# The last two places of a mixture of experts cut to 64 tokens, the tokens' rows read ahead of the last weights, and the sum z kept in PSUM

## The chip, the cores and the metric

The kernel runs on one NeuronCore of one Trainium2 chip. The metric is the device time of one execution in microseconds. TensorE is called PE here, VectorE DVE, ScalarE ACT, GpSimd POOL; SP is SyncE, which issues nearly all of the DMAs.

## What is computed

One encoder block over 512 tokens of width 1024: a layer norm, a token mixer (gated linear attention and differential attention), a second norm, a mixture of experts, a third norm. The change lies in the mixture of experts and the third norm:

```python
logits = xf @ router_w + router_b          # 512 tokens, 32 experts
top_v, top_i = lax.top_k(logits, 4)        # 4 experts for a token
gates = softmax(top_v)
# for each expert, over the tokens that chose it:
g = min(x @ w_gate[e] + b_gate[e], 7)
u = clip(x @ w_up[e] + b_up[e], -7, 7)
a = g * sigmoid(1.702 * g) * (u + 1)
yb = a @ w_down[e] + b_down[e]             # all three weights are 1024 x 1024 f32
y[token] += gate * yb
h = LN2(alpha * h + y)
```

## The kernel before

From about 735 us on, the kernel works through 32 **places**, one expert each. Places 0 and 1 hold experts 0 and 1; the other experts are sorted by their number of tokens and put into places of fitting size. A place has a form (`FORM`, line 32). `None` takes 128 tokens, with weights and tokens split into two fp32r parts and three matmuls a product (L1341 to L1343). `(4, 3)`, `(2, 1)` and `(4, 1)` take 96, 64 and 32 tokens in plain fp32, several small matmuls at once in column tiles of the array (L1351). Place 20 (`WIDE`) takes 128 tokens and 32 more.

A place has three **products**, gate, up and down, of eight steps k each; the step of one place runs gate of e, up of e, down of e-1 (`gate_up`, `down`, `product`). Each product begins with a matmul that adds the bias (L1324 for `None`, L1326 for `(2, 1)`, L1330 for the two others), so these rows mark where products begin. Between the steps lie the transposes ("turns") of the activations `u` into `an` (in gate of e, by the form of e-1) and of the gathered tokens `x` into `xn` (in down of e-1, by the form of e+1).

The weights come as **tiles** of 1 MB, two steps k each: four tiles a product, twelve a place, 384 in all, in the order gate e, up e, down e-1. They are listed in `todo` and issued on SP (`load`, L1015) into 12 slots (11 around place 20). A slot is free when PE has done with its tile (`used`, `free_row`), for a `None` place when the tile has been split. So tile n is issued when tile n-12, one place earlier, has been used. Results of a place are scattered to DRAM by token (`scatter`, tensor `s_y`, four rows for each token), except those of the last two places.

**The end before.** After the weights, `todo` holds eight tiles of 1 MB that read `s_y` back (`yv`): for each of the four blocks b of 128 tokens, the rows of choices 2 and 3 first, then those of 0 and 1. `scaled` adds gate times row into the sum z of the block (DVE L1587, or ACT L1584 and POOL L1585), some while the last product runs (`late`), some through PE (`ON_PE`, L1614, with a diagonal matrix `dg`). The results of places 30 and 31 stay on the chip, split in two parts (`y2`: L1422 on ACT, L1423 on DVE), and `add_back` (L1188) spreads them over the tokens with a 0/1 matrix `w`. `combine` adds PSUM into z (L1615), and `finish` normalises: statistics (L1858), root on ACT (L1860), scale (L1866), the affine part (L1873 to L1878), the output. PSUM is handed out in two rings of four banks, `psb` and `psl`.

## Time and profile before

| | us |
|---|---|
| median of 3 runs | 1827.13 |
| lowest and highest run | 1823.83, 1828.16 |
| the profiled execution, its own time | 1825.93 |
| its span, first to last instruction | 1823.9 |
| PE busy | 1731.9 (95%) |
| DVE busy | 705.8 (39%) |
| weights, queue q1: share of 16 DMA engines | 68.7% |

The table counts a whole execution with stages of different limits; the shares say little about the stage that changes, which begins near 890 us. All times below count from the start of the span. A matmul's row lasts longer than the distance to the next one, since matmuls overlap; the distance between starts is what one costs.

### The profile page before, as it was taken

What the parts mean: (1) busy time and instruction counts of PE and PEld (TensorE: products, weight loads), DVE (VectorE), ACT (ScalarE), POOL (GpSimd) and SP (SyncE); (2) the same over time, 40 slices, a digit from 0 to 9 for tenths busy, and PEclk for the clock granted to TensorE, in tenths of its full rate; (3) what the DMA queues carried; (4) which work ended last, traced back from release to release, by engine and by line L of the source; (5) the groups of instructions that cost most, each with busy time, mean ns of one, the idle gap of its engine ahead of it and who ended that gap; (6) DMA issues with size and microseconds to landing.
All of it is one profiled execution on the core that took longest, in us unless ns stands there. A gap on an engine that the chain in (4) does not pass through costs nothing. (4 is left out here: it accounts for less than half of the span.)

```text
span 1823.9 us, 34470 instructions
## 1 busy us (share of the span) xinstructions
PE 1731.9 (95%) x14456; PEld 1139.2 (62%) x14456; DVE 705.8 (39%) x1055; ACT 571.0 (31%) x947; POOL 478.8 (26%) x399
## 2 busy tenths in 40 slices
PE   6899999899899999899999999999999999999995
PEld 5688887678677788775355554545455454454583
DVE  5337647867673456783000000000004300000598
ACT  5523336555553233562101111011114311101472
POOL 4303415654433023561112211020110101101204
PEclk9999999999999999999999999999999999999998
DMA  7233343113433875489999999999999999999992
GB/s 233 101 116 104 127 128 104 52 52 122 142 130 112 295 271 218 156 293 417 419 418 417 418 419 416 418 412 413 402 401 404 394 378 419 418 420 419 421 421 93
DMA packets 111651, 525.06 MB, mean 288 GB/s; under 512 B 15480, under 2 KB 15920, under 8 KB 61700
## 3 DMA queue, kind: packets, MB, share of 16 engines
q1 hardware_dynamic: 97940, 492.05, 68.7%
q0 software_dynamic: 11248, 26.58, 3.9%
q10 hardware_dynamic: 2304, 4.20, 0.6%
q8 instruction: 115, 1.88, 0.4%
q14 instruction: 44, 0.36, 0.1%
HBM read 490.38 MB, written 37.58 MB: 289 GB/s over the span
## 5 line engine op out<-in xcount | busy, mean ns | idle before, releaser
L1351 PE MATMUL psb<-raw,xn 128*32 128x256 f32 (+1 forms) x6400 | 470.7, 402 | 7.6 <-DMA raw<-in_exp_w_up_dram 3.9
L1351 PEld LDWEIGHTS psb<-raw,xn 128*32 128x32 f32 (+1 forms) x6400 | 222.5, 112 | 207.6 <-issue 69.9
L1367 DVE TENSOR_SCALAR u<-psb 128x512 f32<-128x512 f32 (+1 forms) x51 | 30.5, 599 | 679.4 <-PE psb L1351 679.4
L1351 PE MATMUL psl<-raw,an 128*32 128x256 f32 (+1 forms) x3200 | 241.0, 404 | 3.3 <-DMA raw<-in_exp_w_down_dram 3.3
L1351 PEld LDWEIGHTS psl<-raw,an 128*32 128x32 f32 (+1 forms) x3200 | 109.9, 113 | 99.3 <-issue 34.1
L229 PE MATMUL psb<-hTh,wh 128*128 128x512 f32 x384 | 162.1, 422 | 8.2 <-ACT sg L544 4.0
L1232 POOL DMA_INDIRECT x<-s_h,grows x56 | 57.5, 1028 | 422.9 <-PE psl L1278 396.2
L1049 DVE TENSOR_TENSOR wl<-raw,wh 128x1024 fp32r<-128x1024 f32 x114 | 136.9, 1225 | 48.9 <-ACT wh L1038 18.7
L231 PE MATMUL psb<-hTl,wh 128*128 128x512 f32 x384 | 153.7, 400 | 0.0
L230 PE MATMUL psb<-hTh,wl 128*128 128x512 f32 x384 | 153.0, 398 | 0.0
L1038 ACT CAST wh<-raw 128x1024 fp32r<-128x1024 f32 x114 | 117.7, 1049 | 67.7 <-PE psb L1342 32.5
L1240 POOL DMA_INDIRECT s_y<-y,srows x53 | 53.6, 1012 | 318.6 <-DMA s_y<-y,srows 159.9
L169 ACT CAST wh<-raw 128x1024 fp32r<-128x1024 f32 x88 | 91.8, 1046 | 129.4 <-PE psb L231 81.2
L1279 ACT COPY xn<-psl 128x512 f32<-128x512 f32 (+1 forms) x41 | 20.4, 497 | 341.5 <-PE psl L1278 341.5
L170 POOL TENSOR_TENSOR wl<-raw,wh 128x1024 fp32r<-128x1024 f32 x36 | 91.5, 2540 | 116.7 <-ACT wh L169 82.3
L170 DVE TENSOR_TENSOR wl<-raw,wh 128x1024 fp32r<-128x1024 f32 x52 | 70.1, 1351 | 92.4 <-ACT wh L169 92.4
L229 PEld LDWEIGHTS psb<-hTh,wh 128*128 128x128 f32 x384 | 73.4, 191 | 27.7 <-ACT sg L544 5.1
L230 PEld LDWEIGHTS psb<-hTh,wl 128*128 128x128 f32 x384 | 73.5, 192 | 18.3 <-issue 2.5
L231 PEld LDWEIGHTS psb<-hTl,wh 128*128 128x128 f32 x384 | 73.1, 190 | 18.7 <-DVE hTl L349 0.9
L1279 ACT COPY an<-psl 128x512 f32<-128x512 f32 (+1 forms) x41 | 20.4, 497 | 162.7 <-PE psl L1278 162.7
L1341 PE MATMUL psb<-wh,xh 128*128 128x512 f32 x160 | 66.4, 415 | 1.2 <-ACT wh L1038 1.2
L1343 PE MATMUL psb<-wl,xh 128*128 128x512 f32 x160 | 64.4, 403 | 3.2 <-DVE wl L1049 3.2
(460 smaller groups left out, 2728.8 us busy)
## 6 DMA issues: line engine op xcount, KB each, us to landing
raw<-in_exp_w_up_dram SPq DMA_DIRECT2D x128, 1024.0 KB, 17.3
raw<-in_exp_w_down_dram SPq DMA_DIRECT2D x128, 1024.0 KB, 17.8
raw<-in_exp_w_gate_dram SPq DMA_DIRECT2D x125, 1024.0 KB, 17.0
raw<-in_w_in_dram SPq DMA_DIRECT2D x32, 1024.0 KB, 6.2
s_y<-zero SPq DMA_DIRECT2D x16, 512.0 KB, 8.0
raw<-s_y SPq DMA_DIRECT2D x8, 1024.0 KB, 19.2
raw<-in_w_br_gla_dram SPq DMA_DIRECT2D x4, 1024.0 KB, 6.5
raw<-in_w_br_diff_dram SPq DMA_DIRECT2D x4, 1024.0 KB, 5.6
```

Source lines behind the costliest of these rows:

```text
L169: nc.scalar.copy(h, raw[:, 2 * s:2 * s + 2])
L170: self.low.tensor_sub(l, raw[:, 2 * s:2 * s + 2], h.bitcast(F32))
L229: nc.tensor.matmul(out, lhsT=sh, rhs=mh, start=first, stop=False)
L230: nc.tensor.matmul(out, lhsT=sl, rhs=mh, start=False, stop=False)
L231: nc.tensor.matmul(out, lhsT=sh, rhs=ml, start=False, stop=last)
L1038: nc.scalar.copy(h, src)
L1049: nc.vector.tensor_sub(sub[2], sub[0], sub[1].bitcast(F32))
L1232: self.nc.gpsimd.indirect_dma_start(out=x[:, t * D // n:(t + 1) * D // n], out_offset=None, in_=self.K.d_h1.rearrange("t (n d) -> (t n) d" ...
L1240: self.nc.gpsimd.indirect_dma_start(out=self.K.d_y.rearrange("t (n d) -> (t n) d", n=n), out_offset=bass.IndirectOffsetOnAxis(ap=srow, axi ...
L1341: nc.tensor.matmul(ps[n], lhsT=xh[:, k], rhs=h[:, cs], start=False, stop=False)
L1343: nc.tensor.matmul(ps[n], lhsT=xh[:, k], rhs=l[:, cs], start=False, stop=k == KC - 1)
L1351: nc.tensor.matmul(ps[t * d // T][i * m:i * m + m, t * d % T:t * d % T + d], lhsT=xT[:, o:o + m], rhs=w[:, i * d:(i + 1) * d], start=False ...
```

## The change

1. **Forms.** The two `None` places at the end (30 and 31) become `(2, 1)`, of 64 tokens. The number of places of each form stays: places 11 and 24, which were `(2, 1)`, become `None`, and the places between are dealt out anew.
2. **Reads of `s_y`.** They stand ahead of the last four weight tiles (down of 31), ordered by block. They may be issued once place 29 has been scattered (`y_there`). Each of the eight read tiles is added to z on DVE by two instructions (`add_rows`), four tiles in up of 31, four in down of 30; then its slot is free for a later load.
3. **z in PSUM.** Within the last product PE takes z of a block into PSUM by a matmul with the identity (`fold_z`) and adds the rows of place 30; after the product, those of 31. The norm reads PSUM. The diagonal matrices, `scaled`, `combine` and the adds on POOL go.
4. **Turn of place 31.** It stands inside down of 30, at k = 3, instead of behind it.

```diff
-for _f, _is in (((4, 1), (2, 19, 29)), ((2, 1), (3, 4, 8, 11, 14, 17, 21, 24, 26, 28)),
-                ((4, 3), (5, 6, 7, 9, 10, 12, 13, 15, 16, 18, 22, 23, 25, 27))):
+for _f, _is in (((4, 1), (2, 19, 29)), ((2, 1), (3, 4, 8, 12, 15, 18, 22, 27, 30, 31)),
+                ((4, 3), (5, 6, 7, 9, 10, 13, 14, 16, 17, 21, 23, 25, 26, 28))):
...
+        self.y_at, self.y_there = self.n_w - N_LAST, False
...
-        while self.n_raw < n and self.free:
-            slot = self.slots[self.n_raw] = self.free.pop(0)
+        while self.n_raw < n and self.free and (self.n_raw != self.y_at or self.y_there):
+
+            i = self.n_raw - self.y_at
+            key = self.n_raw if i < 0 else ("y", i) if i < Y_TILES else self.n_raw - Y_TILES
+            slot = self.slots[key] = self.free.pop(0)
...
-        for n in range(2):
-            for i in range(2):
-                self.nc.tensor.matmul(ps[n], lhsT=w[:, b * P:(b + 1) * P], rhs=y[i][:, n * 512:(n + 1) * 512],
+        for i in range(2):
+            for n in range(2):
+                m, cs = (slice(0, P), slice(n * 512, (n + 1) * 512)) if form is None else (slice(n * 64, n * 64 + 64), slice(0, 512))
+                self.nc.tensor.matmul(ps[n], lhsT=w[m, b * P:(b + 1) * P], rhs=y[i][m, cs],
...
+            if e == E - 3:
+                self.y_there = True
+                self.load()
...
+                if e == E - 1 and which == 1 and k in K_Y0:
+                    add_rows(K_Y0.index(k))
...
-                self.todo += [yv[b][:, j:j + 2] for j in (2, 0) for b in range(NB)]
+                self.todo[self.y_at:self.y_at] = [yv[b][:, j:j + 2] for b in range(NB) for j in (0, 2)]
...
+            def add_rows(i):
+
+                b, y = i // 2, self.raws.pop(("y", i))
+                for j in range(2):
+                    n = i % 2 * 2 + j
+                    nc.vector.scalar_tensor_tensor(self.z[b], y[j], self.gates[:, b, n:n + 1], self.z[b], op0=ALU.mult, op1=ALU.add)
+                self.give(self.slots.pop(("y", i)))
...
+                if k in K_Y:
+                    add_rows(4 + K_Y.index(k))
+                if k == K_LAST:
+
+                    aT = left.tile([P, D], F32, tag="al", bufs=1, name="an")
+                    self.turn_form(us[0], aT, FORM[E - 1])
...
-                self.down(aT, before, E - 2, tail, y2[0], gs[0])
-                aT = self.turn(us[0], "a")
+                self.down(aT, before, E - 2, tail, y2[0], gs[0], FORM[E - 2])
...
+        ps = [[self.psb(), self.psb()] for b in range(2)]
+
+        def fold_z(b, n):
+            nc.tensor.matmul(ps[b][n], lhsT=c.ident, rhs=self.z[b][:, n * 512:(n + 1) * 512], start=True, stop=False)
 
         def late(k):
...
+            if k in K_Z:
+                b = K_Z.index(k)
+                if b == 2:
+                    ps.append([self.psl(), self.psl()])
+                for n in range(2):
+                    fold_z(b, n)
+                self.add_back(ps[b], b, w[:, 0], y2[0], False, False, FORM[E - 2])
+
+        self.down(aT, self.ohs[:, :, E - 1:E], E - 1, late, y2[1], gs[1], FORM[E - 1])
+        ps.append([self.psl(), self.psl()])
+        for n in range(2):
+            fold_z(3, n)
+        self.add_back(ps[3], 3, w[:, 0], y2[0], False, False, FORM[E - 2])
         for b in range(NB):
...
+            self.add_back(ps[b], b, w[:, 1], y2[1], False, True, FORM[E - 1])
+        self.finish(out, [left.tile([P, D], F32, tag=t, bufs=1, name="o" + t) for t in ("g", "s", "ah", "al")], ps)
...
+Y_TILES, N_LAST = 8, 4
...
+K_Y0, K_Y, K_LAST, K_Z = (1, 3, 5, 7), (1, 2, 3, 4), 3, (2, 4, 6)
```

Lines move by up to 16 (L1351 becomes L1357, L1188 L1194, L1015 L1019). How the order of the instructions moves, at three places:

PE at the start of place 24, its gate product. `psb` and `psl` are PSUM, `xn` and `xh`, `xl` the turned tokens, `wh`, `wl` the split weights, `an` the turned activations. Before:

```order
L1326 MATMUL psb<-bias,ohg 128x512
L1351 MATMUL psb<-raw,xn 64x512 x8
L1278 MATMUL psl<-tab,u 128x128 x4
L1351 MATMUL psb<-raw,xn 64x512 x4
L1278 MATMUL psl<-tab,u 128x128 x2
```

and now, the first step of the same product:

```order
L1330 MATMUL psb<-bias,ohs 128x512 x2
L1347 MATMUL psb<-wh,xh 128x512
L1348 MATMUL psb<-wh,xl 128x512
L1349 MATMUL psb<-wl,xh 128x512
L1347 MATMUL psb<-wh,xh 128x512
```

Place 24 has become a `None` place in the middle of the run, six matmuls a step in place of two.

SP at the end of the list of loads. Before:

```order
L1015 DMA raw<-in_exp_w_down_dram 128x2048
L1015 DMA raw<-s_y 128x2048 x8
L1874 DMA out_dram<-og 128x1024
L1874 DMA out_dram<-os 128x1024
L1874 DMA out_dram<-oah 128x1024
```

and now (the rows of register arithmetic between the last loads are left out):

```order
L1019 DMA raw<-in_exp_w_down_dram 128x2048
L1019 DMA raw<-s_y 128x2048 x8
...
L1019 DMA raw<-in_exp_w_down_dram 128x2048
...
L1891 DMA out_dram<-og 128x1024
L1891 DMA out_dram<-os 128x1024
```

The eight reads of `s_y` now have the four tiles of down of 31 behind them.

PE from the turn of place 31 to the last add. `y`, `x` are the two parts of place 30's result, `wh`, `wl` those of place 31's. Now:

```order
L1284 MATMUL psl<-tab,u 128x128 x4
L1357 MATMUL psl<-raw,an 64x512 x8
L1332 MATMUL psl<-bias,ohg 128x512
L1357 MATMUL psl<-raw,an 64x512 x6
L1607 MATMUL psb<-z_4743,tab 128x512 x2
L1194 MATMUL psb<-y,w 128x512 x2
L1194 MATMUL psb<-x,w 128x512 x2
L1357 MATMUL psl<-raw,an 64x512 x4
```

The folds of z and the adds of place 30 now lie between the steps of the last product; before, PE had nothing but that product there, and all 32 adds (L1188) behind it.

## Rows read from the trace of the kernel before

**Rows 1.** The page: what the DMA moved in 40 equal slices of the span.

```profile
GB/s 233 101 116 104 127 128 104 52 52 122 142 130 112 295 271 218 156 293 417 419 418 417 418 419 416 418 412 413 402 401 404 394 378 419 418 420 419 421 421 93
```

**Rows 2.** Waits of PE from 893.5 to 1679 us: us in total, times, longest.

```profile
PE psl L1330 <- ACT ohg L1312: 0.5, 1, 0.5
PE psb L1351 <- DMA raw<-in_exp_w_gate_dram: 0.4, 1, 0.4
```

**Rows 3.** Timeline of PE, places 11 to 13: start, us, what; bias rows begin products.

```profile
1106.91 0.50 PE L1326 MATMUL psb<-bias,ohg 128*128 128x512 f32 x1
...
1114.36 0.97 PE L1330 MATMUL psl<-bias,ohg 128*128 128x512 f32 x4
...
1127.13 0.97 PE L1330 MATMUL psb<-bias,ohg 128*128 128x512 f32 x4
...
1139.35 0.97 PE L1330 MATMUL psb<-bias,ohg 128*128 128x512 f32 x4
...
1150.74 0.49 PE L1326 MATMUL psl<-bias,ohg 128*128 128x512 f32 x1
```

**Rows 4.** Timeline of PE, down of 18, and up of place 30.

```profile
1364.60 0.97 PE L1330 MATMUL psl<-bias,ohg 128*128 128x512 f32 x4
...
1377.61 0.73 PE L1324 MATMUL psb<-bias,ohs 128*128 128x512 f32 x2
...
1711.90 0.62 PE L1324 MATMUL psb<-bias,ohs 128*128 128x512 f32 x2
...
1723.28 0.40 PE L1330 MATMUL psl<-bias,ohg 128*128 128x256 f32 x2
```

**Rows 5.** Timeline of SP's issues: tiles of down of 26.

```profile
1605.04 9.49 SPq L1015 DMA_DIRECT2D raw<-in_exp_w_down_dram  x4
```

**Rows 6.** Tiles issued in 1608-1609, 1620-1621, 1459-1476, 1520-1530 us: issue to landing.

```profile
DMA to landing us min/median/max: 17.3/17.3/17.3
...
DMA to landing us min/median/max: 15.8/15.8/15.8
...
DMA to landing us min/median/max: 4.8/7.3/14.0
...
DMA to landing us min/median/max: 10.8/11.2/12.0
```

**Rows 7.** Stretches: engines' busy time (columns PE, PEld, DVE, ACT, POOL), granted clock, DMA.

```profile
1460.00:1470.00 10.00, 10.00 (x164) 5.97 (x160) 0.00 (x0) 1.46 (x3) 1.00 (x1) 1.00 0.65 258
...
1530.00:1540.00 10.00, 10.00 (x47) 3.19 (x43) 0.00 (x0) 0.97 (x2) 1.99 (x2) 1.00 1.01 420
...
1784.00:1786.00 2.00, 1.75 (x8) 1.13 (x6) 1.96 (x2) 2.00 (x3) 1.92 (x2) 1.00 0.22 94
1790.00:1792.00 2.00, 2.00 (x5) 1.61 (x6) 2.00 (x1) 0.00 (x0) 1.92 (x2) 0.50 0.00 0
```

**Rows 8.** The line that adds rows to z on DVE: ns min/median/max.

```profile
L1587 DVE SCALAR_TENSOR_TENSOR z<-raw,gates,z x6: 1274/3250/3428, 1781.8 to 1797.6; 128x1024 f32<-128x1024 f32 x6
```

**Rows 9.** Timeline of PE behind the last product.

```profile
1789.23 0.50 PE L1188 MATMUL psb<-wl,w 128*128 128x512 f32 x1 [3.48 <-DVE wl L1423]
...
1793.88 0.39 PE L1188 MATMUL psl<-x,w 128*128 128x512 f32 x1
1794.11 0.39 PE L1188 MATMUL psl<-y,w 128*128 128x512 f32 x1
...
1797.29 3.59 PE L1614 MATMUL psb<-raw,dg 128*128 128x512 f32 x8
```

**Rows 10.** Timeline of ACT and DVE behind the last product.

```profile
1783.98 1.37 ACT L1422 ACTIVATE wh<-psl,gs 128x512 fp32r<-128x512 f32 x2 [1.84 <-PE psl L1343]
...
1788.43 1.40 DVE L1423 SCALAR_TENSOR_TENSOR wl<-psl,gs,wh 128x512 fp32r<-128x512 f32 x2
...
1800.14 1.28 DVE L1858 BATCH_NORM_STATS2 st<-z 128x6 f32<-128x512 f32 x2
...
1801.58 1.23 DVE L1615 TENSOR_TENSOR z<-z,psb 128x512 f32<-128x512 f32 x2
```

More of the change, by code (lines that the diff above doesn't have):

```diff
@@ L1015, in load @@
             self.nc.sync.dma_start(raw, self.todo[self.n_raw])
-            self.raws[self.n_raw] = [raw[:, k] for k in range(RAW_K)]
+            self.raws[key] = [raw[:, k] for k in range(RAW_K)]
             self.n_raw += 1
@@ L1419, in down @@
             yh, yl = y
-            for n in range(2):
+            for n in range(len(ps)):
                 cs = slice(n * 512, (n + 1) * 512)
@@ L1475, in experts @@
             if e == E - 2:
-                last = [self.pick(self.pm[:, :, j:j + 1], nc.gpsimd) for j in (E - 2, E - 1)]
+                last = [self.pick(self.pm[:, :, j:j + 1], nc.gpsimd, 2) for j in (E - 2, E - 1)]
             def first(which, k):
@@ L1589, in experts @@
         y2.append([left.tile([P, D], F32R, tag=t, bufs=SUBS - i, name=t) for i, t in enumerate(("wh", "wl"))])
-        dg = [left.tile([P, NB, P], F32, tag="pe", bufs=2, name="dg") for _ in range(2)]
+        ps = [[self.psb(), self.psb()] for b in range(2)]
+        def fold_z(b, n):
+            nc.tensor.matmul(ps[b][n], lhsT=c.ident, rhs=self.z[b][:, n * 512:(n + 1) * 512], start=True, stop=False)
         def late(k):
-            if 1 < k < NB + 2:
-                for j in ON_PE[k - 2]:
-                    nc.gpsimd.tensor_scalar_mul(dg[j][:, k - 2], c.ident, g[:, k - 2, j:j + 1])
-            for t in TURNS[k]:
-                scaled(*t)
@@ L1600, in experts @@
-        self.down(aT, self.ohs[:, :, E - 1:E], E - 1, late, y2[1], gs[1])
-        late(KC)
-        ps = [[q(), q()] for q in (self.psb, self.psb, self.psl, self.psl)]
-        for b in range(NB):
-            for i in range(2):
-                self.add_back(ps[b], b, w[:, i], y2[i], i == 0, i == 1 and ON_PE[b] == ())
-        def combine(b):
-            for j in range(2):
-                if j not in ON_PE[b]:
-                    scaled(b, j)
-            for n in range(2):
-                cs = slice(n * 512, (n + 1) * 512)
-                for j in ON_PE[b]:
-                    nc.tensor.matmul(ps[b][n], lhsT=dg[j][:, b], rhs=y_row(b, j)[:, cs], start=False, stop=j == ON_PE[b][-1])
-                nc.vector.tensor_add(z[b][:, cs], z[b][:, cs], ps[b][n])
@@ L1617, in experts @@
-        self.finish(out, [left.tile([P, D], F32, tag=t, bufs=1, name="o" + t) for t in ("g", "s", "ah", "al")], combine)
+            self.tick()
+            if k == 0:
+                nc.scalar.activation(gs[0], c.eps, AF.Sqrt)
+            if k in K_Z:
[5 more added lines that the diff above has]
+                self.add_back(ps[b], b, w[:, 0], y2[0], False, False, FORM[E - 2])
@@ new lines, in experts @@
+        self.down(aT, self.ohs[:, :, E - 1:E], E - 1, late, y2[1], gs[1], FORM[E - 1])
[3 more added lines that the diff above has]
+        self.add_back(ps[3], 3, w[:, 0], y2[0], False, False, FORM[E - 2])
+        for b in range(NB):
+            self.add_back(ps[b], b, w[:, 1], y2[1], False, True, FORM[E - 1])
+        self.finish(out, [left.tile([P, D], F32, tag=t, bufs=1, name="o" + t) for t in ("g", "s", "ah", "al")], ps)
+        for b in range(NB):
+            for n in range(2):
+                nc.scalar.copy(self.z[b][:, n * 512:(n + 1) * 512], ps[b][n])
@@ L1846, in overflow, with finish @@
             with self.tc.tile_pool(name="fin", bufs=1) as self.left:
-                self.finish(out, self.z)
-    def finish(self, out, o, combine=None):
+                self.finish(out, self.z, [[z[:, :512], z[:, 512:]] for z in self.z])
+    def finish(self, out, o, z):
         nc, gb = self.nc, self.K.gb
@@ L1865, in norm @@
                 nc.vector.scalar_tensor_tensor(mv[:, b, 0:1], mv[:, b, 0:1], -1.0, rs[:, b], op0=ALU.mult, op1=ALU.mult)
-                nc.scalar.activation(o[b], self.z[b], AF.Identity, bias=mv[:, b, 0:1], scale=rs[:, b])
+                for n, cs in enumerate(halves):
+                    nc.scalar.activation(o[b][:, cs], z[b][n], AF.Identity, bias=mv[:, b, 0:1], scale=rs[:, b])
         def affine(b):
@@ L1875, in affine @@
             else:
-                nc.vector.scalar_tensor_tensor(o[b], self.z[b], mv[:, b, 0:1], gb[:, 0], op0=ALU.subtract, op1=ALU.mult)
-                for cs in halves:
+                for n, cs in enumerate(halves):
+                    nc.vector.scalar_tensor_tensor(o[b][:, cs], z[b][n], mv[:, b, 0:1], gb[:, 0, cs], op0=ALU.subtract, op1=ALU.mult)
                     nc.vector.scalar_tensor_tensor(o[b][:, cs], o[b][:, cs], rs[:, b], gb[:, 1, cs], op0=ALU.mult, op1=ALU.add)
@@ L1881, in finish @@
         for b in range(NB):
-            if combine is not None:
-                combine(b)
             stats(b)
```

20 lines of the change are left out of this document (4 added, 16 removed).

## The prediction

> **What bounds the kernel now.** Three views were read in this order: the page's slices for the transfers, PE's waits and timeline for the middle of the run, and the timelines of all engines behind the last product. The slices show a stream of weights at about 420 GB/s from slice 19 to the end, with a dent between slices 27 and 36, down to 378 [rows 1]. That looks like a kernel bound by the stream. PE's waits say something more: between 893.5 and 1679 us PE waits 0.9 us in all [rows 2]. So for 785 us both are full. PE works a little behind the stream, and 12 slots keep them together: a tile is issued when PE has used the tile one place earlier. If PE falls back, the time from issue to landing shrinks. It was 17.3 and 15.8 us for tiles issued at 1608.4 and 1620.4; at 10.8 us, near 1525, the stream was still full; where it came down to 4.8 us, near 1469, the stretch moved 258 GB/s [rows 6, 7]. The dent in the slices is made of such places. This is the reader's first point: **how much PE lags at each place decides when the stream can run, and the forms decide the lag.** The second point is the end. The stream is over at about 1785.5 us, 94 GB/s being left in the two microseconds from 1784 [rows 7], and the span ends at 1823.9. These 38.4 us hold no load, only the last sums and the norm.
>
> **The change: forms.** The products' lengths are the distances between bias rows. Up of a `(2, 1)` place: 1114.36 - 1106.91 = 7.45 us; of a `(4, 3)` place: 1150.74 - 1139.35 = 11.39 [rows 3]; of a `None` place: 1723.28 - 1711.90 = 11.38 [rows 4]. Turns come on top: gate of 12 is 12.22, so the turn of a `(2, 1)` place costs 0.83; down of 10, with the turn for a `(4, 3)` place, is 12.77, so 1.38 [rows 3]; down of 18, with the turn for a `None` place, is 13.01, so 1.62 [rows 4]. Now count PE's work up to the gate of 27. Gate and up of places 11 to 26 exchange two `(2, 1)` for two `None`: 2 x 2 x (11.38 - 7.45) = 15.7 us. The downs of 10 to 25 gain two `None` and lose one `(2, 1)` and one `(4, 3)`: 22.8 - 7.5 - 11.4 = 3.9. The turns of both kinds change alike: 2 x (2 x 1.62 - 0.83 - 1.38) = 2.1. PE therefore comes to gate of 27 **21.7 us later**. Over the whole run the counts of forms are equal; the work is done earlier, and the light places come last.
>
> Can the stream hide this? The last tile of down of 26 waits for exactly that point: it is the last of four issued from 1605.04 on, at 1605.04 + 9.49 - 0.33 = 1614.2 [rows 5], and took about 16.5 us to land, between 17.3 and 15.8 [rows 6]. With the new forms it is issued 21.7 us later. The landing can be shortened to 10.8 us at no loss, and to 4.8 us with an almost empty queue [rows 6]. So the stream slips by 21.7 + 10.8 - 16.5 = 16.0 at most and 21.7 + 4.8 - 16.5 = 10.0 at least. Four heavy places (23 to 26) follow one another, which keeps the queue nearly empty, so I take 7.5 us, close to the 7.3 in the middle of the row of 1459 to 1476: **+12.7 us**. From there on places 27 to 31 are lighter than the stream on the whole, and in the stretch it ran at 418 to 421 GB/s before [rows 1], so nothing is caught up. The gathers of places 30 and 31 halve: 2 x 128 rows of 2 KB less, 0.52 MB at 420 GB/s, **-1.2 us**. The scatters of places 11 and 24 grow, while PE is the slower one, at no cost.
>
> **The change: reads ahead of the last weights.** The bytes are the same, so the stream ends no sooner; what ends last is now a weight tile. The wait for place 29's scatter and SP's queue behind it (the other reads, the last four tiles) are covered by the tiles of a whole place in flight. The adds are 16 on DVE, 1.27 us each when POOL is quiet and 3.25 beside POOL's own adds [rows 8]; those adds are gone, so I take 1.3, 2.6 a tile against 2.5 us of stream. In front of DVE's queue stands now a wait for the first read tile, and behind it `u` of place 31. PE needs this `u` in down of 30 at k = 3, and stands idle about 17 us there (from 10 us before the first read tile lands, less the two tiles of four steps, to 11.7 after it: four tiles and `u`). The four last tiles land later still, so this idling is hidden; it comes back as a clock that has to rise.
>
> **The change: the end.** From the landing of the second of the last tiles, 5.0 us before the stream's end, PE does six more steps of 7.45/8 = 0.93: 5.6 us. Three folds lie between them, two fp32 matmuls each at 3.59/4 = 0.90 [rows 9], and three groups of four adds; an add costs 0.23 (1794.11 - 1793.88) [rows 9], a group 0.92, or 0.46 if two halves of the array work side by side. I take 0.7: 3 x 2.5 = 7.5. Behind the product the last bank of `psl` is the one that the product itself used, so the second half of the last fold waits for both parts of the result: 0.69 on ACT and 0.70 on DVE [rows 10] and 0.3 for the hand-overs, 1.7. Then come the fold 0.9, a group 0.7, and the first group of place 31, 0.7: 4.0. Sum 17.1 - 5.0 = 12.1 us behind the stream. For the clock I add 1.4 (bounds 0 and 4, below). Then the norm. Before, it took 23.8 us from the first statistic at 1800.14 to the span's end [rows 10]; three pairs of adds into z at 1.2 go [rows 10], and the halves that the norm is now cut into cost about 0.4: 20.5. The new end is 12.1 + 1.4 + 20.5 = 34.0 us behind the stream, where it was 38.4: **-4.4 us**.
>
> No row shows two adds on 64 partitions side by side. The Trainium skill, page TensorEngine Tiling, section Performance Considerations, gives two row tiles where the contracted dimension is at most 64; by it the five groups would save 1.2 us more than the sum has.
>
> **Sum.** 12.7 - 1.2 - 4.4 = +7.1 us on the profiled execution of 1825.93: **1833 us**. The median of the runs is 1.2 us above that execution; the comparison is with the latter. About 0.3% (5.5 us) is what a measurement of this kernel can tell from no change, that is 1820.4 to 1831.4.
>
> **Rivals.** *A, the sum:* landing between 10.8 and 4.8 us, clock and adds at their bounds: 1828 to 1838. About a third of it lies under 1831.4. *B, the stream doesn't slip:* the slots are free soon enough, as it were if PE's lag were eaten by the dent that is there already. Then the time is 1825.9 - 1.2 - 4.4 = 1820.3, with a spread of 2 to either side. For it speaks that the stream had its dent before, too, and was back at 418 to 421 GB/s behind it [rows 1]; against it, that the margin was only 16.5 - 10.8 = 5.7 us at the deciding tile, and 21.7 are asked for. It decides at gate of 27: a lag of less than 6 us there gives B. *C, the clock:* behind 3.48 us of idle PE the stretch from 1790 to 1792 was granted 0.50, which is 1.2 GHz, and adds came 0.43 apart [rows 7, 9]. After the long idling in down of 30 PE has only some 6 us of work before it waits again. If the lower level lasts through the last product, its 17 us of work take some 8 us more: 1841. *D, DVE stays slow:* at 3.25 us an add the sixteen adds take 52 us, 31 more, and the result of place 30 and the folds behind them wait: about 1858. Against it: POOL has nothing there.
>
> The Trainium skill, page TensorE: Matmul & The Clock Gate, section "HAM oscillation", describes C as a loop that waits for DMA between short bursts and runs each burst at half the clock; the one row at 0.50 agrees, no row shows it for a train of such waits.
>
> **How the numbers follow.** A has 0.65, B 0.20, C 0.11, D 0.04. Faster by over 0.3%: half of B, 0.10. Within 0.3%: the other half and a third of A, trimmed to 0.20: 0.30. Slower: 0.45 of A, C and D: 0.60. The range runs from 1820 to 1840; outside lie part of B, half of C, and D, under 0.2.
>
> **What would show it.** Right, if gate of 27 begins near 1636 (1614 before), the slices from 1540 to 1640 sink under 400 GB/s, and the stream ends near 1797. The tail is right if 34 us follow. Wrong in the first step, if the stream ends near 1785; in the second, if DVE's adds exceed 1.5 us each or the granted clock in the last 40 us is mostly 0.5; in the third, if the first statistic doesn't follow the stream's end by some 13.5 us.

## The result: 0.9% slower, and beyond the range

The changed kernel takes **1843.59 us** in the median (1841.77 to 1844.98), the kernel before, beside it, 1827.64. The ratio is **1.0089**, with an interval of 1.0069 to 1.0108: 13 to 20 us more. A second set of runs on another chip gave 1.0088 (1.0069 to 1.0108). The forecast was 1833 us, range 1820 to 1840. The direction was right, with 0.60 on it; the size was not: less than half of the loss was forecast.

The page of the changed kernel shows a dent close to where one was forecast, and others long ahead of it: slice 36 (1612 to 1658 us) has 357 GB/s, and from slice 25 on (1105 us) every second slice or so goes down to 395, 383, 370, 371, 357, where the kernel before had one shallow dent with 378 at its bottom [rows 1]. The row is what the DMA moved in 40 slices of the span:

```profile
GB/s 237 93 115 103 126 126 103 52 75 99 170 120 152 306 286 202 87 374 419 419 418 419 417 419 395 418 383 418 370 415 371 357 377 418 415 357 418 421 421 120
```

PE's waits behind 893 us are now 26 us in all, where there was next to nothing up to 1679 [rows 2]. The four largest (us in total, times, longest):

```profile
PE psl L1284 <- DVE u L1374: 15.8, 1, 15.8
PE psl L1336 <- ACT ohg L1318: 4.7, 1, 4.7
PE psl L1357 <- DMA raw<-in_exp_w_down_dram: 3.1, 4, 1.4
PE psb L1357 <- DMA raw<-in_exp_w_up_dram: 1.6, 3, 0.6
```

The first row is the idling in down of 30 that the prediction named ("about 17 us"). The second stands at place 20, where it was 0.5 us before [rows 2].

Two lengths are used from here on, for every kernel alike. The **stream** runs from the start of gate of 5 (893.91 us in the kernel before) to the point, near the end, from which a whole microsecond passes with less than 10 GB/s on the DMA; what the DMA moves later are mainly the outputs. The **tail** is what follows, to the span's end. The stretch before place 5 has the same work in all kernels, and took 889.6 to 901.8 us in the fifteen profiled executions; counting from gate of 5 takes this out. The last microseconds of the stream before, in stretches of one microsecond (length, busy time of PE, PEld, DVE, ACT, POOL, granted clock, DMA share, GB/s):

```profile
1785.00:1786.00 1.00, 0.75 (x4) 0.29 (x2) 0.96 (x2) 1.00 (x2) 1.00 (x1) 1.00 0.10 41
1786.00:1787.00 1.00, 0.00 (x0) 0.00 (x0) 1.00 (x1) 1.00 (x2) 1.00 (x1) 1.00 0.00 0
```

and after:

```profile
1805.00:1806.00 1.00, 1.00 (x8) 0.35 (x8) 0.00 (x0) 0.00 (x0) 0.00 (x0) 1.00 0.18 74
1806.00:1807.00 1.00, 1.00 (x8) 0.16 (x4) 0.00 (x0) 0.00 (x0) 0.00 (x0) 1.00 0.00 0
```

So the stream took 1786.0 - 893.91 = 892.1 us before and 1806.0 - 891.35 = 914.7 after; the tail 37.9 and 35.8. The difference of the spans, 1841.8 - 1823.9 = 17.9, is made of **+22.6 stream, -2.1 tail**, and -2.6 from the stretch ahead. The forecast had +11.5 and -4.4.

The changed kernel's tail, from the timeline of all engines (start, us, engine):

```profile
1779.43 10.40 DVE L1532 SCALAR_TENSOR_TENSOR z<-raw,gates,z 128x1024 f32<-128x1024 f32 x8 [37.55 <-DMA raw<-s_y]
...
1791.39 1.10 PE L1284 MATMUL psl<-tab,u 128*128 128x128 f32 x4 [15.85 <-DVE u L1374]
...
1801.80 1.08 PE L1357 MATMUL psl<-raw,an 128*64 128x512 f32 x4 [0.46 <-DMA raw<-in_exp_w_down_dram]
...
1816.93 1.13 PE L1607 MATMUL psl<-z,tab 128*128 128x512 f32 x2 [0.52 <-DVE wl L1429]
...
1818.56 0.39 PE L1194 MATMUL psb<-wh,w 64*128 64x512 f32 x2
...
1818.79 0.40 PE L1194 MATMUL psb<-wl,w 64*128 64x512 f32 x2
...
1819.21 1.29 DVE L1874 BATCH_NORM_STATS2 st<-psb 128x6 f32<-128x512 f32 x2 [2.34 <-PE psb L1194]
```

Each of the adds on DVE took 10.40/8 = 1.30 us. PE's first 15.85 us of waiting end with `u` of place 31, which stands on DVE behind eight adds. From 1801.80 on PE has no more than half a microsecond of waiting until the first statistic, 13.2 us behind the stream.

### The profile page after: what moved, and what is told of

Read it like the earlier page. It is cut to its first block, busy times and chain, and to the rows that moved or that the text cites. A ratio compares the mean times of both kernels' runs of the same rounds, so it can differ in the third digit from the quotient of the medians.

```text
span 1841.8 us, 34425 instructions
## 1 busy us (share of the span) xinstructions
PE 1735.2 (94%) x14448; PEld 1142.2 (62%) x14448; DVE 704.6 (38%) x1056; ACT 571.0 (31%) x955; POOL 464.9 (25%) x389
## 4 chain that ended last, share of the span: by engine, by line
PE 68%; DVE 12%; DMA 11%; ACT 4%; issue 2%; POOL 2%; SPq 0%; ACTq 0%; DVEq 0%; POOLq 0%
PE psb L1357 22%; PE psl L1357 11%; PE psb L229 5%; PE psb L230 5%; PE psb L231 5%; DMA raw<-in_exp_w_down_dram 3%; DMA raw<-in_exp_w_up_dram 2%; PE psl L1284 2%; DMA raw<-in_exp_w_gate_dram 2%; PE psb L1347 2%; PE psb L1349 2%; PE psb L1348 2%; PE psb L1336 1%; DVE kl L623 1%; DMA raw<-s_y 1%
## 5 line engine op out<-in xcount | busy, mean ns | idle before, releaser
L1357 PE MATMUL psb<-raw,xn 128*32 128x256 f32 (+1 forms) x6400 | 472.8, 403 | 6.9 <-DMA raw<-in_exp_w_gate_dram 3.5
L1357 PEld LDWEIGHTS psb<-raw,xn 128*32 128x32 f32 (+1 forms) x6400 | 223.0, 113 | 210.0 <-issue 69.1
L1357 PE MATMUL psl<-raw,an 128*32 128x256 f32 (+1 forms) x3200 | 247.6, 406 | 5.7 <-DMA raw<-in_exp_w_down_dram 3.9
L1357 PEld LDWEIGHTS psl<-raw,an 128*32 128x32 f32 (+1 forms) x3200 | 113.1, 113 | 105.2 <-issue 40.1
L1053 DVE TENSOR_TENSOR wl<-raw,wh 128x1024 fp32r<-128x1024 f32 x114 | 137.9, 1225 | 68.1 <-PE psb L1349 21.6
L230 PEld LDWEIGHTS psb<-hTh,wl 128*128 128x128 f32 x384 | 74.3, 193 | 18.2 <-issue 2.2
```

Source lines behind the costliest of these rows:

```text
L230: nc.tensor.matmul(out, lhsT=sl, rhs=mh, start=False, stop=False)
L1053: nc.vector.tensor_sub(sub[2], sub[0], sub[1].bitcast(F32))
L1357: nc.tensor.matmul(ps[t * d // T][i * m:i * m + m, t * d % T:t * d % T + d], lhsT=xT[:, o:o + m], rhs=w[:, i * d:(i + 1) * d], start=False ...
```

## The experiments

Thirteen further runs were made, one of them the changed kernel again. All ratios are to the kernel before on the same chip, in the same job; stream and tail (us) come from one trace each.

| run | stream | tail | ratio | interval |
|---|---|---|---|---|
| before | 892.1 | 37.9 | | |
| after | 914.7 | 35.8 | 1.0089 | 1.0069 to 1.0108 |
| after_again | 913.2 | 35.5 | 1.0088 | 1.0069 to 1.0108 |
| two_more | 909.4 | 35.3 | 1.0073 | 1.0055 to 1.0091 |
| u_first | 908.0 | 37.2 | 1.0067 | 1.0050 to 1.0084 |
| folds_early | 912.3 | 32.9 | 1.0066 | 1.0041 to 1.0090 |
| reads_last | 909.0 | 41.2 | 1.0092 | 1.0068 to 1.0116 |
| forms_alone | 908.6 | 25.6 | 1.0005 | 0.9988 to 1.0022 |
| rest_alone | 891.1 | 60.6 | 1.0122 | 1.0102 to 1.0143 |
| none_at_28 | 892.7 | 36.0 | 0.9981 | 0.9964 to 0.9997 |
| folds_early_28 | 896.2 | 33.1 | 0.9967 | 0.9950 to 0.9984 |
| reads_last_28 | 894.2 | 45.5 | 1.0041 | 1.0027 to 1.0056 |
| adds_ahead_28 | 894.7 | 33.9 | 0.9986 | 0.9969 to 1.0004 |
| old_tail_28 | 896.4 | 25.5 | 0.9933 | 0.9913 to 0.9953 |
| old_tail_28_two | 896.8 | 25.7 | 0.9933 | 0.9917 to 0.9949 |

Read the columns one by one. **The stream's length goes with the order of the forms**: 891 to 892 with the old order, 893 to 897 with the 128-token places at 28 and 29, 908 to 915 with the new order, whatever the tail does (up to 5 us of these spreads are the long products of the last part of this section). **The tail's length goes with what stands behind the stream.** The runs that show each come first, in pairs.

### The forms alone, and all but the forms

**forms_alone** is the kernel before with the new order of forms, and what two places of 64 tokens at the end need to be added back:

```diff
-for _f, _is in (((4, 1), (2, 19, 29)), ((2, 1), (3, 4, 8, 11, 14, 17, 21, 24, 26, 28)),
+for _f, _is in (((4, 1), (2, 19, 29)), ((2, 1), (3, 4, 8, 12, 15, 18, 22, 27, 30, 31)),
...
-                aT = self.turn(us[0], "a")
+                aT = self.place("a", FORM[E - 1])
+                self.turn_form(us[0], aT, FORM[E - 1])
+                self.tick()
```

> The kernel before with the new order of forms and nothing else: reads of s_y behind the weights, z in SBUF, the turn of place 31 behind down of 30. Theory 'lag' (the None places moved to 11 and 24 hold the slots of the stream): the stream's last byte 18 to 21 us later than before, near 1805, gate of 27 at 1641 to 1644, and a tail of about 34 to 38 us behind it: 1840 to 1845 us. Theory 'reads' (the reads ahead of the last weights, or the wait for place 29's scatter, hold the stream): nothing of it is in this kernel, so the stream ends near 1786 and the time is 1820 to 1828 us.

Measured: 1827.29 against 1825.53 us, no difference that can be told. Both theories fall, each by half: the time is the one of 'reads', the stream the one of 'lag'. The stream is 16.5 us longer, as 'lag' had it, and its last bytes come at 1801 (stretches of one microsecond, columns as above):

```profile
1800.00:1801.00 1.00, 1.00 (x3) 0.39 (x3) 0.96 (x2) 0.00 (x0) 0.00 (x0) 1.00 0.06 25
1801.00:1802.00 1.00, 1.00 (x4) 0.41 (x3) 0.90 (x2) 0.00 (x0) 0.00 (x0) 1.00 0.00 0
```

But the first statistic follows 2.0 us behind the stream's end, where it took 14 before (1800.14 [rows 10] less 1786.0). The timeline of all engines, from the first matmul behind the last product on:

```profile
1783.31 0.51 PE L1190 MATMUL psb<-y,w 64*128 64x512 f32 x2
...
1792.58 0.80 PE L1190 MATMUL psb<-wl,w 64*128 64x512 f32 x2 [5.35 <-DVE wl L1425]
...
1803.02 1.28 DVE L1862 BATCH_NORM_STATS2 st<-z 128x6 f32<-128x512 f32 x2
```

The tail is 25.6 us instead of 37.9. So **the old tail was not a length that follows the stream**. With two places of 128 tokens at the end, the last product ended with the stream (ACT takes up its result at 1783.98 [rows 10], the stream ended at 1786.0); with places of 64 tokens it ends some 18 us ahead of the stream, and what follows it runs while the reads still arrive. The new forms lengthen the stream by 16.5 and shorten the old tail by 12.3.

**rest_alone** is the other half: the changed kernel with the old order of forms. Part 4 goes with it: the turn of place 31 stands behind down of 30 again.

```diff
-for _f, _is in (((4, 1), (2, 19, 29)), ((2, 1), (3, 4, 8, 12, 15, 18, 22, 27, 30, 31)),
+for _f, _is in (((4, 1), (2, 19, 29)), ((2, 1), (3, 4, 8, 11, 14, 17, 21, 24, 26, 28)),
...
-                if k == K_LAST:
...
+                aT = self.turn(us[0], "a")
```

> The changed kernel with the old order of forms: the last two places take 128 tokens, the reads stand ahead of the last weights, z is folded in PSUM. Theory 'lag': the stream ends within 2 us of 1786 as before, and PE is late rather than the stream: down of 31 starts at about 1773, has 12.5 us and three folds of 2.7 between its steps, one more and the adds behind it, first statistic near 1799, 22.6 us to the end: 1821 to 1826 us. Theory 'reads': the stream ends near 1805 as in the changed kernel, 1838 to 1846 us.

Measured: 1848.11 us, ratio 1.0122, outside both. The stream ends as before (891.1), so the reads ahead of the last weights don't hold it, and 'reads' is out. 'Lag' was right on the stream and wrong on what PE does then. PE's waits behind 880 us:

```profile
PE psb L1349 <- DVE wl L1053: 14.3, 4, 10.7
PE psl L1349 <- DVE wl L1053: 8.3, 6, 3.3
```

and DVE's timeline, in up of 31:

```profile
1748.29 1.23 DVE L1053 TENSOR_TENSOR wl<-raw,wh 128x1024 fp32r<-128x1024 f32 x1 [0.53 <-ACT s L1366]
1759.65 2.60 DVE L1532 SCALAR_TENSOR_TENSOR z<-raw,gates,z 128x1024 f32<-128x1024 f32 x2 [10.14 <-DMA raw<-s_y]
1762.17 2.35 DVE L1053 TENSOR_TENSOR wl<-raw,wh 128x1024 fp32r<-128x1024 f32 x2
```

A `None` place needs DVE for the second part of each weight tile (`wl`, L1053). The first add of rows (L1532) stands in DVE's queue ahead of the next split and waits 10.14 us for its tile from DRAM. PE waits 10.7 us for the split behind it, and 8.3 in down of 30, where the other adds stand between the splits; 3.6 of the 22.6 us come ahead of all adds (the kernel before has 2.1 us of such waits). With DVE's queue in this order, the reads ahead of the last weights don't go with 128-token places at the end: parts 1 and 2 of the change belong together. Their effects don't add: +0.05% alone, +1.2% alone, +0.9% together.

### The places of the heavy forms

**none_at_28** is the changed kernel with the old order up to place 25; the two `None` places stand at 28 and 29, ahead of the two of 64 tokens.

```diff
-for _f, _is in (((4, 1), (2, 19, 29)), ((2, 1), (3, 4, 8, 12, 15, 18, 22, 27, 30, 31)),
-                ((4, 3), (5, 6, 7, 9, 10, 13, 14, 16, 17, 21, 23, 25, 26, 28))):
+for _f, _is in (((4, 1), (2, 19, 27)), ((2, 1), (3, 4, 8, 11, 14, 17, 21, 24, 30, 31)),
+                ((4, 3), (5, 6, 7, 9, 10, 12, 13, 15, 16, 18, 22, 23, 25, 26))):
```

> The changed kernel, but its forms are those of before up to place 25; then 26 takes 96, 27 takes 32, 28 and 29 take 128, 30 and 31 take 64 tokens. The same counts. Theory 'lag': PE falls back so late that the slots cost the stream little: last byte at 1786 to 1791, the tail of 35.8 us as in the changed kernel, 1823 to 1829 us. Theory 'light end' (two places of 64 tokens at the end leave PE without cover, wherever the heavy ones stand): the stream ends after 1800, 1838 us or more.

Measured: 1822.69 us, ratio 0.9981, and a stream of 892.7 with the tail of the changed kernel, 36.0. Its slices:

```profile
GB/s 250 83 116 104 127 127 104 52 52 122 145 126 111 280 267 225 169 280 417 417 418 417 418 419 417 417 412 417 396 403 407 391 381 418 418 414 420 421 421 112
```

'Lag' holds: the same counts of forms, dealt out otherwise, give the 16 us of forms_alone back. This is rival B of the prediction, a stream that doesn't slip, made by hand: B had 5.6 us less than before, and 0.0019 x 1825.5 = 3.5 are measured.

### What part of the tail counts

**u_first** puts `u` of place 31 ahead of all adds on DVE.

```diff
-                    add_rows(4 + K_Y.index(k))
+                    add_rows(K_Y.index(k))
...
-K_Y0, K_Y, K_LAST, K_Z = (1, 3, 5, 7), (1, 2, 3, 4), 3, (2, 4, 6)
+K_Y0, K_Y, K_LAST, K_Z = (), (0, 1, 2, 3, 4, 5, 6, 7), 3, (2, 4, 6)
```

> The changed kernel with u of place 31 ahead of all sixteen adds on DVE, so that PE turns it at once and does all of down of 30 without the wait of 15.85 us. Theory 'hidden' (what ends last is the landing of the last tiles and PE's work between them; the first of these tiles lands at 1799 either way): 1842 to 1844.5 us. Theory 'exposed' (the wait pushes the tail): 6 to 9 us less, 1835 to 1838. Theory 'clock' (PE now stands idle just ahead of the last product and does it at 1.2 GHz): 3 to 8 us more, 1846 to 1852.

Measured: 1838.14 us, ratio 1.0067. By the time alone 'exposed' comes nearest. The two columns say otherwise: the tail is not shorter but 1.4 us longer, 37.2, and it is the stream that is 6.7 shorter, in a stretch where both kernels have the same instructions (why, the last part of this section says). In the tail 'hidden' holds: the wait has moved from down of 30 to the first tile of the last product. PE's waits:

```profile
PE psl L1357 <- DMA raw<-in_exp_w_down_dram: 21.6, 4, 19.2
```

Behind 19.2 us of idle PE the granted clock was 0.50 (1.2 GHz) in the first five microseconds of work, and 0.92 in the next (columns as above):

```profile
1790.00:1795.00 5.00, 3.92 (x10) 1.37 (x12) 2.43 (x3) 0.20 (x1) 0.00 (x0) 0.50 1.02 421
1795.00:1800.00 5.00, 5.00 (x18) 1.46 (x16) 0.00 (x0) 0.00 (x0) 0.00 (x0) 0.92 0.29 120
1800.00:1805.00 5.00, 5.00 (x20) 1.46 (x16) 0.00 (x0) 0.00 (x0) 0.00 (x0) 1.00 0.00 0
```

The first three steps of the product took 5.1 us there (1791.08 to 1796.14 in PE's timeline) and 3.4 in the changed kernel (1799.41 to 1802.81, with a wait of 0.46 between). That is about what the 1.4 us are made of. The Trainium skill, page TensorE: Matmul & The Clock Gate, section "HAM oscillation", has a loop that waits for DMA and runs each burst at half the clock. Here the trace agrees for the first burst only; in the work that follows PE has the folds between the tiles, and the clock was back at 1.00 from 1800 on.

**folds_early** goes further: `u` first, then four tiles of adds, then the second part of place 30's result, then the other four; the folds of blocks 0 and 1 stand ahead of the last product, half of block 3's at k = 6.

```diff
+                for i in range(4, Y_TILES):
+                    add_rows(i)
...
-            if k in K_Z:
-                b = K_Z.index(k)
+        for b in range(2):
+            fold(b)
```

> The changed kernel with u of place 31 first on DVE, then four tiles of adds, the second part of place 30's result, the other four tiles; the folds of blocks 0 and 1 and place 30's rows for them ahead of the last product, in the time in which PE waits for its first tile; the fold of block 2 at k = 2, half of block 3's at k = 6. Theory 'PE's work behind the last tiles': two groups of 2.5 us and a fold of 0.9 leave the stretch behind the stream's end, first statistic 6 to 8 us behind it where it was 13 to 14.5: 1830 to 1834 us if its stretch ahead has no long products, 4 to 5 more if it has. Theory 'clock' (PE idles at 1.2 GHz more often): no gain, 1837 to 1843 us.

Measured: ratio 1.0066. This kernel has the long products (below), as after_again has, which ran beside it: 4.5 us less than that one, of which the tail gives 2.6. The first statistic comes 10.3 us behind the stream (1810), not 6 to 8. The timeline shows why:

```profile
1802.83 5.39 PE L1357 MATMUL psl<-raw,an 128*64 128x512 f32 x12 [3.54 <-DMA raw<-in_exp_w_down_dram]
...
1820.33 1.29 DVE L1882 BATCH_NORM_STATS2 st<-psb 128x6 f32<-128x512 f32 x2 [2.34 <-PE psb L1194]
```

The three steps that follow the wait take 5.39 us, where three take 2.9 at full clock (1.94/2 a step); the granted clock was 0.50 from 1803 to 1808. So 'PE's work' is right and 'clock' takes about half of its gain. **folds_early_28** is the same with the `None` places at 28 and 29:

> The same early folds with the forms of the run with the 128-token places at 28 and 29. Theory 'PE's work behind the last tiles': stream's end at 1788 to 1791, first statistic 6 to 8 us behind it, 22.6 us of norm: 1815 to 1820 us. Theory 'clock': no gain over that run's 1822.7 us.

Measured: ratio 0.9967, where none_at_28 had 0.9981. The two intervals overlap, so the time decides nothing here. The first statistic comes 10.5 us behind the stream, as in folds_early and not 6 to 8; the tail is 2.9 us shorter than that of none_at_28, and the stream 3.5 longer, with five long products of its own.

**reads_last** keeps z in PSUM but puts the reads behind the weights again, block by block, with the rows of places 30 and 31 already in PSUM:

```diff
-        self.y_at, self.y_there = self.n_w - N_LAST, False
+        self.y_at, self.y_there = self.n_w, False
...
+        def combine(b):
+            for i in (2 * b, 2 * b + 1):
+                add_rows(i)
+            for n in range(2):
+                nc.tensor.matmul(ps[b][n], lhsT=c.ident, rhs=self.z[b][:, n * 512:(n + 1) * 512], start=False, stop=True)
```

> The changed kernel with its eight reads of s_y behind the weights again, as in the kernel before, in the new order by block; z is still summed in PSUM: the rows of places 30 and 31 go in first, then, block by block, eight adds' worth of rows on DVE, the fold with the identity, the statistics. Theory 'reads ahead' (the loss of the changed kernel lies in its last weight tiles: two steps of product, folds, adds and the whole norm stand behind the stream's end, 36 us in all): adds and norm of blocks 0 to 2 run while the last reads arrive, DVE has 8.1 us a block from about 17 us ahead of the stream's end and some 5 us at the end, so 18 to 23 us behind the stream, 1820 to 1830 us. Theory 'PSUM' (the folds and the norm from PSUM are what is slow): 1838 us or more.

> The same with the 128-token places at 28 and 29. Theory 'reads ahead': stream's end at 1788 to 1792, 18 to 23 us behind it, 1808 to 1815 us. Theory 'PSUM': no better than that run's 0.998 of the kernel before.

Measured: 1.0092 (1842.77 us) and 1.0041, tails of 41.2 and 45.5. Both times are those of 'PSUM', but neither theory named what happens. DVE's timeline of reads_last, blocks 0 and 1, and PE's fold of block 1:

```profile
1785.93 5.24 DVE L1532 SCALAR_TENSOR_TENSOR z<-raw,gates,z 128x1024 f32<-128x1024 f32 x4
1793.10 0.70 DVE L1872 BATCH_NORM_STATS2 st<-psb 128x6 f32<-128x512 f32 x1 [1.93 <-PE psb L1625]
1794.80 0.70 DVE L1872 BATCH_NORM_STATS2 st<-psb 128x6 f32<-128x512 f32 x1 [1.01 <-PE psb L1625]
...
1795.66 5.19 DVE L1532 SCALAR_TENSOR_TENSOR z<-raw,gates,z 128x1024 f32<-128x1024 f32 x4
...
1800.91 3.78 PE L1625 MATMUL psb<-z,tab 128*128 128x512 f32 x4 [6.14 <-DVE z L1532]
```

The statistics of a block wait for its fold on PE, the adds of the next block wait behind them, and the fold of the next block waits for these: a round trip of some 10 us a block (1785.93 to 1795.66), with neither engine full. A part of it is PE's clock, of which neither theory spoke: behind 6.14 us without work the fold took 3.78 us, where the same four instructions took 1.98 in the changed kernel (1802.81) at a granted 1.00; from 1801 to 1806 it was 0.59 here. **adds_ahead_28** puts the adds of a block ahead of the statistics of the block before:

```diff
-                combine(b)
+                for i in ((0, 1) if b == 0 else (b + 1,)):
+                    if i < NB:
+                        combine(i)
```

> The run with the reads behind the weights and the 128-token places at 28 and 29, with one difference: on DVE the adds of a block stand ahead of the statistics of the block before, so that DVE doesn't wait for the fold on PE. Theory 'round trip' (DVE waited 2 + 1 us for the fold in each of four blocks, and what stood behind it waited too): some 10 to 20 us less than that run, ratio 0.992 to 0.998. Theory 'DVE is full' (its adds take twice as long while POOL works, and the blocks cost 8 us each anyway): under 5 us less, ratio over 1.001.

Measured: ratio 0.9986, 0.55% or 10 us less than reads_last_28 and just outside the 0.998 of 'round trip'. Against the tail of old_tail_28 (25.5, below) reads_last_28 lost 20.0 us, and 11.6 of them come back: the round trip was most of it. How the 8.4 that stay come about was not traced. One slow part is DVE's last four adds, 9.15 us where four take 5.19 with POOL quiet:

```profile
1786.49 5.19 DVE L1532 SCALAR_TENSOR_TENSOR z<-raw,gates,z 128x1024 f32<-128x1024 f32 x4
...
1793.27 9.15 DVE L1532 SCALAR_TENSOR_TENSOR z<-raw,gates,z 128x1024 f32<-128x1024 f32 x4
...
1794.91 6.42 POOL L1888 TENSOR_TENSOR og<-og,gb 128x1024 f32<-128x1024 f32 x2 [55.21 <-ACT og L1881]
```

POOL multiplies and adds for the norm of block 0 in that time (third row). It is the slow add of [rows 8] again. The Trainium skill, page SBUF — State Buffer, section "SBUF: two separate sides", describes a port pair that DVE and GpSimd lock against each other; the two durations, 5.19 and 9.15, go its way.

**old_tail_28** is forms_alone with the `None` places at 28 and 29: the old reads, the old adds, z in SBUF.

> The kernel before, its own tail (reads of s_y behind the weights, adds on DVE, ACT and POOL, z in SBUF), with the forms of the run with the 128-token places at 28 and 29 and 64 tokens at 30 and 31. Theory 'order of the tail' (behind the stream the old tail needs 2 us to the first statistic when the stream ends late, the new one 13; forms cost only where the stream slips): the stream ends at 1788 to 1791 and the time is 1813 to 1819 us. Theory 'PE ends it' (the old end is bound by PE's work, not by the reads): 1822 to 1828 us.

Measured: 1820.08 against 1831.90 us, **ratio 0.9933** (0.9913 to 0.9953). Tail 25.5, stream 896.4. 'Order of the tail' holds: the ranges were given for a chip on which the kernel before takes 1825.5 us, and 0.9933 of that is 1813. It is the best of all and beats both kernels. With the reads at the end of the stream, only adds and the norm follow; with weights at the end, steps of a product, folds and adds follow, and then the same norm. Parts 2 to 4 of the change cost 35.8 - 25.6 = 10 us against the old tail, when both have two places of 64 tokens at the end.

### Products that take 1.2 us longer

Four products of the changed kernel (down of 6, 10, 13 and 25) took 13.3 to 13.5 us; in u_first and forms_alone, which have the same instructions there, 12.1 or 12.2. **after_again** asked whether this was chance.

> The changed kernel itself once more, beside the others, because four of its products (down of 6, 10, 13 and 25) took 1.2 us longer in its first trace than the same products in the two kernels that have the same code there. Theory 'chance' (an event of that execution): without them, span 4 to 5 us shorter, 1837 to 1840 us. Theory 'code' (the layout of this program): they are there again, 1842 to 1845 us.

Measured: ratio 1.0088, and the same four products are long. Down of 25 in the first trace, from PE's timeline (from its bias to the next):

```profile
1628.99 0.97 PE L1336 MATMUL psl<-bias,ohg 128*128 128x512 f32 x4
...
1633.29 9.21 PE L1357 MATMUL psl<-raw,an 128*32 128x256 f32 x144
1642.44 0.51 PE L1332 MATMUL psb<-bias,ohg 128*128 128x512 f32 x1
```

**two_more** adds two transposes, far behind:

```diff
-        for b in range(NB):
+        for b in (0, 0, 1, 2, 3):
             nc.tensor.transpose(pt[:, b * P:(b + 1) * P], pe[:, b], c.ident)
```

> The changed kernel with two more transposes of 0.14 us on PE (one block turned twice in each of the two preparations ahead of down of 31), far behind the four products that take 1.2 us longer in it (down of 6, 10, 13, 25). Theory 'layout' (where the program's instructions lie decides whether PE runs short of them there): the long products vanish or move to others; if they vanish, 4 to 6 us less, ratio to the kernel before 1.005 to 1.007. Theory 'data and timing' (something that these products do with their neighbours): the same four long products, 1.008 to 1.011.

Measured: 1837.35 us, ratio 1.0073, and no long product. The same stretch:

```profile
1623.06 0.97 PE L1336 MATMUL psl<-bias,ohg 128*128 128x512 f32 x4
...
1627.36 7.98 PE L1357 MATMUL psl<-raw,an 128*32 128x256 f32 x144
1635.27 0.50 PE L1332 MATMUL psb<-bias,ohg 128*128 128x512 f32 x1
```

13.45 there and 12.21 here, with identical instructions around. So 914.7 - 909.4 = 5.3 us of the stream, about a third of the loss, come with something that two instructions elsewhere in the program change. **old_tail_28_two** made the same edit in another kernel that has such products:

> The kernel with the old tail and the 128-token places at 28 and 29 (ratio 0.9933), whose trace has five products longer by 1.1, 1.1, 0.3, 1.1 and 1.1 us than the same products in other kernels, with the two further transposes of the run two_more. Theory 'layout': other instructions behind them move the places at which PE runs short, and the long products go or change: without them 4 to 5 us less, ratio 0.990 to 0.992. Theory 'these forms': the same five, 0.993 to 0.995.

Measured: ratio 0.9933 as without, and the same five long products. The edit doesn't always help. Shown is this: six of the fifteen traces have such products (the changed kernel in both of its own), always at the same places for the same order of forms; nine have none, among them kernels with the same order. Each of them is the down of a 96-token place that holds the turn for a 64-token place, though not every such down is long. So they don't come from the instructions around them alone, and not from chance. PE's weight loads have pauses there in which they wait for nothing that the profile shows, in down of 6 three of 0.3 to 0.6 us. Late loads of instructions are not what these traces show: the profile has such loads as a queue of its own (q8, 16 KB each), and within 3 us of the pauses in down of 6 it has none in any of the six. Which property of the program decides stays open.

## Why the prediction missed, step by step

**What bounds the kernel: right.** PE's lag holds the slots and these hold the stream; the forms set the lag. forms_alone and none_at_28 show it from both sides. Of the signs that the prediction named, the gate of 27 came at 1642.44 for 1636, the stream's end at 1806 for 1797, the tail at 35.8 us for 34; the slices sank, but earlier than from 1540 to 1640, and that is where the miss began.

**The lag at gate of 27: 21.7 forecast, 25.5 measured** where no long products disturb (two_more: 1635.27 - 889.58, against 1614.06 - 893.91 before). The work itself came to 19.9; the turns were over-counted by 1.8 (beside a `None` product a turn for 96 tokens took 0.9 and not 1.38). But **5.6 us are the gate of place 20**, 24.59 instead of 18.97 us, and that is the step that failed. The prediction summed PE's work as if PE never waited. The `None` place at 11 had made the stream slip before, and behind the light places 18 and 19 PE came to place 20 ahead of its first tile. ACT of the kernel before, then ACT and PE of the changed kernel:

```profile
1373.27 2.00 ACT L1038 CAST wh<-raw 128x1024 fp32r<-128x1024 f32 x2 [3.62 <-DMA raw<-in_exp_w_gate_dram]
```

```profile
1378.24 1.99 ACT L1042 CAST wh<-raw 128x1024 fp32r<-128x1024 f32 x2 [5.52 <-DMA raw<-in_exp_w_gate_dram]
...
1381.09 1.99 ACT L1042 CAST wh<-raw 128x1024 fp32r<-128x1024 f32 x2 [0.38 <-DMA raw<-in_exp_w_gate_dram]
1382.99 0.50 ACT L1318 ACTIVATE ohg<-quarters,oh 128x256 fp32r<-128x256 f32 x1
```

```profile
1378.09 0.73 PE L1330 MATMUL psb<-bias,ohs 128*128 128x512 f32 x2
1383.55 0.80 PE L1336 MATMUL psl<-bias,ohg 128*128 128x256 f32 x2 [4.72 <-ACT ohg L1318]
```

ACT starts to split when the tile is there, the bias pattern `ohg` of the place's second part waits behind the splits, and PE's clock falls in the wait (0.66 in this stretch, columns as above):

```profile
1380.00:1390.00 10.00, 6.45 (x30) 3.74 (x30) 5.72 (x8) 5.24 (x8) 1.03 (x1) 0.66 1.01 412
```

Counted from gate of 5, the first split of place 20 starts 3.7 us later in two_more than before (1372.64 - 889.58 against 1373.27 - 893.91), while PE is there 0.6 us earlier (1372.73 - 889.58 against 1377.61 - 893.91 [rows 4]): its wait grew from 0.5 to 4.7 us, and the lower clock behind it makes up the rest of the 5.6. The gate of 20 took 23.8 to 25.2 us in all seven traces with the new order and 18.2 to 20.0 in the other eight. No run took this wait away by itself.

The sign stood in [rows 2]: one of the two waits in 785 us, 0.5 us for this very `ohg`. It was passed over as nothing. It said that at place 20 the stream was just in time.

**The landing at the deciding tile: right.** 7.5 us was taken, between 4.8 and 10.8. In two_more that tile is issued at 1635.40, and the tiles issued from 1626 to 1640 around it took 6.8 and 8.7 (kind, count, KB, us to landing):

```profile
raw<-in_exp_w_down_dram SPq DMA_DIRECT2D x4, 1024.0 KB, 6.8
raw<-in_exp_w_gate_dram SPq DMA_DIRECT2D x2, 1024.0 KB, 8.7
```

About 7.8, then, and by the prediction's own formula 25.5 + 7.8 - 16.5 = 16.8 us of slip; the stream of two_more is 17.3 longer than before. The formula was good; one of its inputs wasn't. That the halved gathers give 1.2 us back is not to be seen at this resolution.

**The reads ahead: right in the parts.** SP's queue cost nothing (the stream keeps 424 GB/s from 1780 to 1790), the adds took 1.30 us, the wait in down of 30 15.85 for a forecast of 17, and it was hidden, as u_first's tail shows. Rival D is out.

**The end: right to the first statistic, in part by luck, and wrong behind it.** 13.5 us behind the stream were forecast, 13.2 measured. PE's work from the second of the last tiles on took 17.4 us (1801.80 to 1819.21) for 17.1, so this sum was good. But the tile was there 4.2 us ahead of the stream's end and not 5.0, and the 1.4 us for the clock did not come; these two cancel. Adds on 64 partitions did run side by side: two of them, one for each half, take 0.23 us together (1818.56, 1818.79 above), where one took 0.23 [rows 9]. The Trainium skill, page TensorEngine Tiling (Array Packing), section Performance Considerations, has two row tiles for a contracted dimension of 64; the trace agrees. A group between the steps took 0.67 us all the same (1804.72 to 1805.39), close to the 0.7 of the sum. The norm took 22.6 us instead of 20.5. Up to the affine part of `oah` it became shorter by 3.7 us, about the 3.3 of the forecast (1800.14 to 1812.42 before, 1819.21 to 1827.82 now). Behind that it became longer, which the forecast did not have: DVE's two instructions for `oah` took 6.20 us instead of 4.53, with POOL at work until 1832.94 beside them (before until 1814.61), and what follows them took 0.8 more. Before and now:

```profile
1812.42 4.53 DVE L1873 TENSOR_TENSOR oah<-oah,gb 128x1024 f32<-128x1024 f32 x2 [0.16 <-ACTq L1843]
```

```profile
1827.82 6.20 DVE L1890 TENSOR_TENSOR oah<-oah,gb 128x1024 f32<-128x1024 f32 x2 [0.31 <-ACT oah L1883]
```

That POOL is what slowed them fits with the adds of adds_ahead_28; no run tried it here. Rival C did not come, and its price of 8 us was too low: at 0.50 adds came 0.43 us apart for 0.23 [rows 7, 9], which makes 17 us of such work nearly twice as long. Here the clock was at 0.50 behind the long wait and back at 1.00 for the last tiles (columns as above):

```profile
1790.00:1795.00 5.00, 3.61 (x10) 1.50 (x12) 4.82 (x5) 0.58 (x1) 0.00 (x0) 0.50 1.02 423
...
1800.00:1805.00 5.00, 4.54 (x18) 1.35 (x15) 2.18 (x3) 0.94 (x2) 0.00 (x0) 1.00 0.72 300
```

**What -4.4 us meant.** The sum was made right, new end against old end. But the text set the old tail against the new as if the reads ahead had earned the difference. The runs show that the light forms earned 12.3 us and the reads ahead with the fold lost 10.2 of them. The prediction didn't ask of the old tail what it asked of the new one: which of its work would remain if the stream ended later.

**The size.** From +7.1 to the +17.9 of the two profiled executions: +5.8 on the stream without long products (17.3 for 11.5: the wait at place 20, less the turns, and what the formula leaves out), +5.3 with them, which no row before showed, +2.3 on the tail, -2.6 from the stretch ahead of place 5: 10.8 in all. Without the long products the ratio is 1.0073 (two_more); on the 1825.93 us against which the forecast was made that is 1839, just inside the range. So by this estimate the time left the range through two things at once, the wait at place 20 and the long products; with either one alone it would have stayed inside.

## What to carry to other kernels

Where two things run full at once, a wait of half a microsecond marks a place where the margin is nil: a slip made ahead of it comes out there, so follow a delay to the first such place, not only to the last. A tail is not a constant that follows the last transfer: ask which of its work is waiting for that transfer and which would be done anyway. Heavy steps late, light steps last, and at the stream's end the data with the least work behind it: that order gave 0.67% here, from the parts of a change that as a whole lost 0.9%.

## What was not expected of the hardware

Products of the same instructions took 1.1 to 1.2 us longer in some programs and not in others; four or five of them make 0.3% of this kernel. Two kernels that differ by less than that, in code that lies elsewhere, can't be told apart by their times alone; the lengths of the stretches can tell them apart, since the other products from up of 5 to up of 17 agreed to 0.03 us in kernels with the same order of forms.
